# Gate tiles dealt earlier and tied behind the weight tiles, their sums begun as the bias, and one tile for the high parts of the merged output

## The chip, the cores and the metric

The kernel runs on one core of a Trainium2 chip. The metric is the time of one execution on the device in microseconds. Three runs of the kernel before took 822.36 to 823.37 us, with a median of 822.74 us.

## The reference

One decoder layer over a sequence of 256 tokens with 2048 channels, in float32. An input vector c gives a shift, a scale and a gate; the normalised input goes through a wide projection; two token mixers run beside each other; their outputs are projected, merged and projected out:

```python
ada = c @ w_ada + b_ada
shift, scale, gate = jnp.split(ada, 3, axis=-1)
h = rms_norm(x, g_pre) * (1.0 + scale[:, None, :]) + shift[:, None, :]
proj = h @ w_in                                    # 2048 x 11824
(qa, kc, vc, ks, vs, kw, vw, ga, za, qb, kb, vb, zb, ma, mb) = jnp.split(proj, IN_SPLITS, axis=-1)
oa = nsa_attention(...)                            # mixer A: 16 heads of 64, three branches
ya = (oa * jax.nn.silu(za)) @ w_br_a               # 1024 x 2048
ob = dilated_mixture(...)                          # mixer B: 8 heads of 128
yb = (ob * jax.nn.silu(zb)) @ w_br_b               # 1024 x 2048
merged = jax.nn.sigmoid(ma) * ya + jax.nn.sigmoid(mb) * yb
out = merged @ w_out                               # 2048 x 2048
return x + gate[:, None, :] * rms_norm(out, g_post)
```

The change touches three places of it: gate (a third of c @ w_ada + b_ada, needed only at the end), merged as an operand of the last product, and the loads of g_post and x for the last line.

## The kernel before

**Products in two parts.** Each float32 operand of a large product is split into a high part and a low part, which TensorE multiplies in its fp32r type: high by high, low by high, high by low. Of the weights ScalarE writes the high part (wH) and VectorE the low part (wL = raw - wH), lines 490 and 491.

**Items.** All weights are cut into items, tiles of 512 KB in most stages, in one list in the order in which TensorE uses them: the passes of the input projection (its last panels are ma and mb, 512 columns each), then the branch stage (w_br_a and w_br_b in turn, one quarter of the columns after the other), then w_out. An item of 512 columns and 256 rows is 12 products of 128x512. `dma(i)` asks for an item's tile on SyncE's queue, in one of seven buffers (raw); `prep(i)` writes wH and wL, three items ahead of the products in `main(i)`. Each prepared item asks for the tile seven further on.

**Gate items.** The gate vector is not a product on TensorE: 32 tiles of w_ada (two halves of 1024 columns, 16 tiles each) are multiplied on VectorE by c, one number per partition, and summed in gacc0 and gacc1 (lines 509 and 511). The first tile of a half is written by a TENSOR_SCALAR, the 15 others are added by a SCALAR_TENSOR_TENSOR. `spread` deals these items between the weight items from `late` on, here from the last four items of mb. When a half is done, GpSimd adds the bias (bg) to its first row (line 1142); near the end a product with ones sums gacc over the partitions (g_ps), and the result is multiplied into gp, the copies of g_post in all partitions.

**The side work.** Attention and everything else that is no item is a generator, `side_main`, of which a step is taken at each weight item. `need` makes it run on to a named point. mixer B's softmaxes lie in it (lines 1040 to 1080), then y, the mixers' outputs times their SiLU gates, split in yH and yL. In the branch stage it takes the merged quarters: for each quarter and each half of the tokens (t) TensorE transposes four blocks into a PSUM buffer, m_ps (one buffer, line 1115), ScalarE copies the high parts (mH, line 1121), and VectorE writes the low parts (mL, line 1122). Here mH lies in seven tiles (`Parts`, of 1 to 4 blocks each) and mL in one. Then ScalarE issues the loads of gp, bg and xr (x again, for the residual), lines 1132 to 1136.

**What sets the order.** The program is written in this order, but the instructions of each engine are then placed by a scheduler, which puts each as early as it expects its inputs. `behind(...)` (tc.issue_after) keeps an instruction in its place behind others. Each engine's queue is then fixed: an instruction that waits holds up all that stand behind it on its engine.

Of the kernel before, what the change touches and what calls it, by code (L numbers as in the profile page):

```python
# [48 lines left out]
def _build(ctx, tc, x, c, positions, w_ada, b_ada, g_pre, g_post, w_in, pe_ck, pe_cv, w_ck1, w_ck2,  # L49
# [396 lines left out]
    late = len(items) - 4  # L446
# [31 lines left out]
    gacc = {}  # L478

    def prep(i):  # L480
# [5 lines left out]
        if it.kind in ("w", "ck"):  # L486
# [4 lines left out]
            V.tensor_tensor(L, raw, H.bitcast(F32), op=OP.subtract)  # L491
            it.H, it.L = H, L
            return
        if it.kind == "ada":
            if it.kt0 == 0:
                accs[it.piece] = ST[:, len(accs) % 2].rearrange("p (h n) -> p h n", h=2)
            acc = accs[it.piece][:, :, :it.n // 2]
        else:
            if it.half not in gacc:
                need("A")  # L500
                gacc[it.half] = big.tile([128, 1024], F32, name=f"gacc{it.half}", tag=("cv", "k2")[it.half])
            acc = gacc[it.half]
        with behind(*(first_h if i < 8 else ())):
            for j in range(it.nk):
# [3 lines left out]
                if it.kt0 + j == 0:  # L508
# [194 lines left out]
    def side_main():  # L703
# [320 lines left out]

        while ("vb", 512) not in done:
            yield
# [76 lines left out]
        mH, mL = Parts(), big.tile([128, KT, S], F32R, name="mL", tag="xH")  # L1103
        for a, b in groups:
            mH.put(lows(a, b, "mH", F32R), a, b)
        yT["m"] = (mH, mL)
        for p in range(4):
# [4 lines left out]
            for t in range(NT):  # L1112
# [3 lines left out]
                ts = slice(t * 128, (t + 1) * 128)  # L1116
                for a, b in groups:
                    a, b = max(a, 4 * p), min(b, 4 * p + 4)
                    if a < b:
                        dH, o = mH.at[a]  # L1120
                        A.activation(dH[:, a - o:b - o, ts], ps[:, a - 4 * p:b - 4 * p], AF.Copy, scale=0.5)
                        V.scalar_tensor_tensor(mL[:, a:b, ts], ps[:, a - 4 * p:b - 4 * p], 0.5,
                                               dH[:, a - o:b - o, ts].bitcast(F32), op0=OP.mult, op1=OP.subtract)
                if t == NT - 1:
                    done.add(("mT", p))
                yield
# [5 lines left out]
        A.dma_start(gp, bass.AP(tensor=g_post.tensor, offset=g_post.offset, ap=[[0, 128], [1, D]]))  # L1132
        bg = big.tile([1, D], F32, name="bg", tag="qb")
        A.dma_start(bg, b_ada[0:1, 2 * D:3 * D])
        for t in range(NT):
            A.dma_start(fin["x"][:, t, :], x[0, t * 128:(t + 1) * 128, :])
# [3 lines left out]
        for half in range(2):  # L1140
            ga = gacc[half]
            G.tensor_tensor(ga[0:1, :], ga[0:1, :], bg[:, half * 1024:(half + 1) * 1024], op=OP.add)
# [89 lines left out]
```

## Time and profile before

| | |
|---|---|
| median of three runs | 822.74 us |
| the profiled execution, its own time | 823.46 us |
| its span, first to last instruction | 821.6 us |
| busy in the span: TensorE | 791.5 us, 96% |
| VectorE | 688.7 us, 84% |
| ScalarE | 417.3 us, 51% |
| GpSimd | 92.0 us, 11% |
| mean granted TensorE clock | 0.994 of full speed |
| traffic of the DMA engines | 193.26 MB, 235 GB/s on average |

In the rows PE is TensorE, PEld its weight loads, DVE VectorE, ACT ScalarE, POOL GpSimd and SP SyncE, whose queue issues the tile loads; a q behind the name is the engine's queue of instructions that don't compute. L560 is line 560 of the kernel. An instruction is named by what it writes and reads: wL<-raw,wH writes wL. The mb panels run from about 520 to 630 us, the branch stage from there to 722 us, w_out from there to 812 us. A wait that the rows name is idle time of that engine before the instruction, with what ended it.

### The profile page before, as it was taken

The page shows a single profiled execution, that of the slowest core. Times are in us where ns is not written, and L with a number is a line of the kernel's source. Part 1 is how long each engine was busy: PE and PEld are TensorE (multiplying, and loading weights), DVE is VectorE, ACT ScalarE, POOL GpSimd, SP SyncE. Part 2 cuts the span into 40 slices and gives each one's busy share as a digit, 9 for nine tenths or more (in the row PEclk, how much of TensorE's full clock was granted, in tenths as well). Part 3 has the DMA queues.
Part 4 walks back from the last instruction along what each step waited for, and adds up shares of the span by engine and source line. Part 5 has one row for each costly group of instructions (what it writes and reads, how often), then busy time and mean ns, then how long its engine had stood idle before and what let it go on. Part 6 is the DMA issues. An engine that isn't in the chain of part 4 may idle for free.

```text
span 821.6 us, 11929 instructions
## 1 busy us (share of the span) xinstructions
PE 791.5 (96%) x4160; PEld 665.9 (81%) x4160; DVE 688.7 (84%) x1068; ACT 417.3 (51%) x684; POOL 92.0 (11%) x111
## 2 busy tenths in 40 slices
PE   5999999999999999999999999999999999999995
PEld 4587888899888888888889999888878878888884
DVE  4899999999997979898888998867568999967455
ACT  2763363433334656576766666556644344445441
POOL 4200000000000036054511120011000010100000
PEclk9999999999999999999999999999999999999998
DMA  9999899989798558744444436554469989986633
GB/s 327 289 349 316 262 332 308 344 295 347 256 337 294 172 160 281 233 122 144 136 141 120 141 113 180 179 154 130 152 237 358 334 290 342 335 272 228 191 101 103
DMA packets 106950, 193.26 MB, mean 235 GB/s; under 512 B 7593, under 2 KB 36617, under 8 KB 106249
## 3 DMA queue, kind: packets, MB, share of 16 engines
q1 hardware_dynamic: 105376, 189.17, 69.5%
q10 hardware_dynamic: 1514, 3.33, 1.1%
q8 instruction: 33, 0.54, 0.3%
q14 instruction: 27, 0.22, 0.1%
HBM read 190.38 MB, written 2.10 MB: 234 GB/s over the span
## 4 chain that ended last, share of the span: by engine, by line
PE 84%; DVE 10%; issue 3%; DMA 2%; ACT 1%; DVEq 0%; ACTq 0%; SPq 0%
PE mm L560 21%; PE mm L561 21%; PE mm L563 21%; DVE wL L491 3%; PE mm L555 3%; PE mm L552 3%; PE mm L550 3%; PE mm L542 2%; PE pt_ps L923 1%; DVE ST L511 1%; PE sA L887 1%; DMA raw<-in_w_ada_dram 1%; PE ada_ps L184 1%; DMA xs<-in_x_dram 1%; PE pvb_ps L1058 1%
## 5 line engine op out<-in xcount | busy, mean ns | idle before, releaser
L490 ACT ACTIVATE wH<-raw 128x1024 fp32r<-128x1024 f32 (+2 forms) x268 | 267.4, 1000 | 293.0 <-PE mm L561 186.5
L491 DVE TENSOR_TENSOR wL<-raw,wH 128x1024 fp32r<-128x1024 f32 (+2 forms) x268 | 316.9, 1186 | 75.5 <-ACT wH L490 70.9
L560 PE MATMUL mm<-wH,xH 128*128 128x512 f32 (+2 forms) x616 | 237.8, 389 | 1.3 <-DVE KB L633 1.1
L561 PE MATMUL mm<-wH,xL 128*128 128x512 f32 (+2 forms) x616 | 235.0, 383 | 0.0
L563 PE MATMUL mm<-wL,xH 128*128 128x512 f32 (+2 forms) x616 | 188.6, 383 | 1.8 <-DVE wL L491 1.8
L560 PEld LDWEIGHTS mm<-wH,xH 128*128 128x128 f32 x616 | 116.1, 189 | 23.1 <-issue 2.7
L563 PEld LDWEIGHTS mm<-wL,xH 128*128 128x128 f32 x616 | 113.7, 189 | 24.2 <-DVE wL L491 2.5
L561 PEld LDWEIGHTS mm<-wH,xL 128*128 128x128 f32 x616 | 116.3, 189 | 20.5 <-DVE xL L246 0.3
L511 DVE SCALAR_TENSOR_TENSOR ST<-raw,vecT,ST 128x768 f32<-128x768 f32 (+2 forms) x75 | 75.9, 1013 | 1.3 <-DMA raw<-in_w_ada_dram 0.9
L550 PE MATMUL mm<-xH,wH 128*128 128x256 f32 x240 | 62.2, 280 | 1.1 <-DVE VB L633 1.1
L552 PE MATMUL mm<-xL,wH 128*128 128x256 f32 x240 | 61.7, 278 | 0.0
L560 PE MATMUL mm<-wH,yH 128*128 128x512 f32 x128 | 50.2, 392 | 0.0
L561 PE MATMUL mm<-wH,yL 128*128 128x512 f32 x128 | 50.0, 390 | 0.0
L561 PE MATMUL mm<-wH,mL 128*128 128x512 f32 x128 | 49.9, 390 | 0.0
L560 PE MATMUL mm<-wH,mH 128*128 128x512 f32 x128 | 49.9, 390 | 0.0
L555 PE MATMUL mm<-xH,wL 128*128 128x256 f32 x240 | 49.1, 280 | 0.6 <-DVE wL L491 0.6
L550 PEld LDWEIGHTS mm<-xH,wH 128*128 128x128 f32 x240 | 45.0, 188 | 1.7 <-issue 1.7
L511 DVE SCALAR_TENSOR_TENSOR gacc<-raw,vecT,gacc 128x1024 f32<-128x1024 f32 x30 | 38.3, 1278 | 8.9 <-DMA raw<-in_w_ada_dram 8.9
L552 PEld LDWEIGHTS mm<-xL,wH 128*128 128x128 f32 x240 | 45.0, 188 | 0.0
L563 PE MATMUL mm<-wL,mH 128*128 128x512 f32 x128 | 39.8, 389 | 0.0
L563 PE MATMUL mm<-wL,yH 128*128 128x512 f32 x128 | 39.5, 390 | 0.0
L555 PEld LDWEIGHTS mm<-xH,wL 128*128 128x128 f32 x240 | 37.0, 188 | 1.0 <-DVE wL L491 1.0
(296 smaller groups left out, 1002.4 us busy)
## 6 DMA issues: line engine op xcount, KB each, us to landing
raw<-in_w_in_dram SPq DMA_DIRECT2D x165, 512.0 KB, 4.2
raw<-in_w_ada_dram SPq DMA_DIRECT2D x48, 512.0 KB, 5.6
raw<-in_w_ada_dram SPq DMA_DIRECT2D x48, 384.0 KB, 4.7
raw<-in_w_out_dram SPq DMA_DIRECT2D x32, 512.0 KB, 4.8
raw<-in_w_br_a_dram SPq DMA_DIRECT2D x16, 512.0 KB, 5.7
raw<-in_w_br_b_dram SPq DMA_DIRECT2D x16, 512.0 KB, 5.9
raw<-in_w_in_dram SPq DMA_DIRECT2D x29, 256.0 KB, 2.7
raw<-in_w_ada_dram SPq DMA_DIRECT2D x24, 256.0 KB, 4.8
```

Source lines behind the costliest of these rows:

```text
L184: T.matmul(ada0[:, half, j, :], lhsT=raws0[q][:, kk, half, j * 128:(j + 1) * 128], rhs=cT[:, kt:kt + 1].to_broadcast([128, 128]), start=(k ...
L490: A.activation(H, raw, AF.Copy)
L491: V.tensor_tensor(L, raw, H.bitcast(F32), op=OP.subtract)
L511: V.scalar_tensor_tensor(acc, r, cc, acc, op0=OP.mult, op1=OP.add)
L542: T.matmul(job.ps[t][:, :job.n], lhsT=hj[:, t * 128:(t + 1) * 128], rhs=it.raw[:, j, cs], start=(first and j == 0), stop=(last and j == it ...
L550: T.matmul(ps, lhsT=it.H[:, j, bs], rhs=sH[:, it.kt0 + j, :], start=(first and j == 0 and b == 0), stop=False, skip_group_check=True)
L552: T.matmul(ps, lhsT=it.H[:, j, bs], rhs=sL[:, it.kt0 + j, :], start=False, stop=False, skip_group_check=True)
L555: T.matmul(ps, lhsT=it.L[:, j, bs], rhs=sH[:, it.kt0 + j, :], start=False, stop=(last and j == it.nk - 1), skip_group_check=True)
L560: T.matmul(ps, lhsT=sH[:, it.kt0 + j, ts], rhs=it.H[:, j, cs], start=(first and j == 0), stop=False)
L561: T.matmul(ps, lhsT=sL[:, it.kt0 + j, ts], rhs=it.H[:, j, cs], start=False, stop=False)
L563: T.matmul(ps, lhsT=sH[:, it.kt0 + j, ts], rhs=it.L[:, j, cs], start=False, stop=(last and j == it.nk - 1))
L887: T.matmul(o, lhsT=QT[:, u.t, h // 2, h % 2, :], rhs=KTt[:, hl, :, 0:128] if u.t == 0 else KTt[:, hl, u.br, :], start=(hl == 0), stop=(hl ...
```

## The change

Four things change.

- The gate items are dealt from 24 items before the end of the projection on, which is the second panel of mb, instead of from the last 4 items. The 32 tiles then lie between 56 weight items, before between 36.
- Each gate sum is kept behind the last wL that was written before it (`lowest`).
- gacc0 and gacc1 are cleared on GpSimd after mixer A, and the bias is loaded into their first rows; all 32 sums are then SCALAR_TENSOR_TENSOR, and GpSimd's two bias adds and the tile bg are gone.
- The high parts of merged are one tile, copied by one instruction for four blocks; the low parts lie in the seven tiles. The load of gp is kept behind the high part of the second quarter, that of xr behind that of the fourth.

```diff
@@ -443,7 +443,7 @@
                 it.kind, it.which, it.q, it.nk, it.n = "ck", n - 3, q, 4, 256
                 it.src = rows((w_ck1, w_cv1)[n - 3][0], 4 * q, 4, 0, 256)
                 items.append(it)
-    late = len(items) - 4
+    late = len(items) - 24
 
     yT = {}
     ws = []
@@ -476,6 +476,7 @@
             DMA.dma_start(it.raw, it.src)
 
     gacc = {}
+    lowest = [None]
 
     def prep(i):
         it = items[i]
@@ -488,7 +489,7 @@
             H, L = (wp.tile([128, 1152], F32R, name="w" + x, tag="w" + x, bufs=3)[:, o:o + it.nk * it.n].rearrange(
                 "p (k n) -> p k n", k=it.nk) for x in "HL")
             A.activation(H, raw, AF.Copy)
-            V.tensor_tensor(L, raw, H.bitcast(F32), op=OP.subtract)
+            lowest[0] = V.tensor_tensor(L, raw, H.bitcast(F32), op=OP.subtract)
             it.H, it.L = H, L
             return
         if it.kind == "ada":
@@ -496,16 +497,14 @@
                 accs[it.piece] = ST[:, len(accs) % 2].rearrange("p (h n) -> p h n", h=2)
             acc = accs[it.piece][:, :, :it.n // 2]
         else:
-            if it.half not in gacc:
-                need("A")
-                gacc[it.half] = big.tile([128, 1024], F32, name=f"gacc{it.half}", tag=("cv", "k2")[it.half])
+            need("gacc")
             acc = gacc[it.half]
-        with behind(*(first_h if i < 8 else ())):
+        with behind(*(first_h if i < 8 else lowest if it.kind == "gate" else ())):
             for j in range(it.nk):
                 cc, r = cT[:, it.kt0 + j:it.kt0 + j + 1], raw[:, j, :]
                 if it.kind == "ada":
                     r = r.rearrange("p (h n) -> p h n", h=2)
-                if it.kt0 + j == 0:
+                if it.kt0 + j == 0 and it.kind == "ada":
                     V.tensor_scalar(acc, r, cc, None, op0=OP.mult)
                 else:
                     V.scalar_tensor_tensor(acc, r, cc, acc, op0=OP.mult, op1=OP.add)
@@ -1022,6 +1021,12 @@
                 V.tensor_tensor(d, ps[:, :, t, :], d, op=OP.add)
             yield
 
+        for half in range(2):
+            gacc[half] = big.tile([128, 1024], F32, name=f"gacc{half}", tag=("cv", "k2")[half])
+            G.memset(gacc[half], 0.0)
+            A.dma_start(gacc[half][0:1, :], b_ada[0:1, 2 * D + half * 1024:2 * D + (half + 1) * 1024])
+        done.add("gacc")
+
         while ("vb", 512) not in done:
             yield
         for t in range(NT):
@@ -1100,9 +1105,10 @@
 
         while ("merged", 0) not in done:
             yield
-        mH, mL = Parts(), big.tile([128, KT, S], F32R, name="mL", tag="xH")
+        mH, mL = big.tile([128, KT, S], F32R, name="mH", tag="xH"), Parts()
         for a, b in groups:
-            mH.put(lows(a, b, "mH", F32R), a, b)
+            mL.put(lows(a, b, "mL", F32R), a, b)
+        turned = []
         yT["m"] = (mH, mL)
         for p in range(4):
             while ("merged", p) not in done:
@@ -1114,32 +1120,33 @@
                 for j in range(4):
                     T.transpose(ps[:, j, :], MA[:, t, (4 * p + j) * 128:(4 * p + j + 1) * 128], ident)
                 ts = slice(t * 128, (t + 1) * 128)
+                dH = mH[:, 4 * p:4 * p + 4, ts]
+                last = A.activation(dH, ps, AF.Copy, scale=0.5)
                 for a, b in groups:
                     a, b = max(a, 4 * p), min(b, 4 * p + 4)
                     if a < b:
-                        dH, o = mH.at[a]
-                        A.activation(dH[:, a - o:b - o, ts], ps[:, a - 4 * p:b - 4 * p], AF.Copy, scale=0.5)
-                        V.scalar_tensor_tensor(mL[:, a:b, ts], ps[:, a - 4 * p:b - 4 * p], 0.5,
-                                               dH[:, a - o:b - o, ts].bitcast(F32), op0=OP.mult, op1=OP.subtract)
+                        dL, o = mL.at[a]
+                        V.scalar_tensor_tensor(dL[:, a - o:b - o, ts], ps[:, a - 4 * p:b - 4 * p], 0.5,
+                                               dH[:, a - 4 * p:b - 4 * p].bitcast(F32), op0=OP.mult, op1=OP.subtract)
                 if t == NT - 1:
                     done.add(("mT", p))
+                    turned.append(last)
                 yield
 
         fin["o"] = big.tile([128, NT, D], F32, name="og", tag="mb")
         fin["x"] = big.tile([128, NT, D], F32, name="xr", tag="ma")
         fin["ssq"] = const.tile([128, NT, 4], F32, name="ssq2")
         gp = big.tile([128, D], F32, name="gp", tag="zb")
-        A.dma_start(gp, bass.AP(tensor=g_post.tensor, offset=g_post.offset, ap=[[0, 128], [1, D]]))
-        bg = big.tile([1, D], F32, name="bg", tag="qb")
-        A.dma_start(bg, b_ada[0:1, 2 * D:3 * D])
-        for t in range(NT):
-            A.dma_start(fin["x"][:, t, :], x[0, t * 128:(t + 1) * 128, :])
+        with behind(turned[1]):
+            A.dma_start(gp, bass.AP(tensor=g_post.tensor, offset=g_post.offset, ap=[[0, 128], [1, D]]))
+        with behind(turned[3]):
+            for t in range(NT):
+                A.dma_start(fin["x"][:, t, :], x[0, t * 128:(t + 1) * 128, :])
         yield
         while "gate" not in done:
             yield
         for half in range(2):
             ga = gacc[half]
-            G.tensor_tensor(ga[0:1, :], ga[0:1, :], bg[:, half * 1024:(half + 1) * 1024], op=OP.add)
             gH, gL = (wp.tile([128, 1152], F32R, name="g" + v, tag="w" + v, bufs=3)[:, :1024] for v in "HL")
             A.activation(gH, ga, AF.Copy)
             V.tensor_tensor(gL, ga, gH.bitcast(F32), op=OP.subtract)
```

Three places show how the instructions move. The first is VectorE's queue at the end of the mb panels. gacc0 is the gate's first half, wL a low part of a weight tile, yL a low part of a mixer's output; raw buffers have higher numbers the later they were asked for. Before:

```order
L509 TENSOR_SCALAR gacc0_6339<-raw_6188,vecT_98 128x1024
L1097 SCALAR_TENSOR_TENSOR yL1_6335<-ZB_178,yH1_6334 128x512 x3
L491 TENSOR_TENSOR wL_6227<-raw_6068,wH_6226 128x1024
L491 TENSOR_TENSOR wL_6250<-raw_6086,wH_6249 128x1024
L511 SCALAR_TENSOR_TENSOR gacc0_6339<-raw_6230,vecT_98,gacc0_6339 128x1024
L491 TENSOR_TENSOR wL_6271<-raw_6119,wH_6270 128x1024
L511 SCALAR_TENSOR_TENSOR gacc0_6339<-raw_6274,vecT_98,gacc0_6339 128x1024
L491 TENSOR_TENSOR wL_6294<-raw_6139,wH_6293 128x1024
L491 TENSOR_TENSOR wL_6317<-raw_6170,wH_6316 128x1024
```

And in the changed kernel:

```order
L492 TENSOR_TENSOR wL_6324<-raw_6230,wH_6323 128x1024
L1102 SCALAR_TENSOR_TENSOR yL1_6389<-ZB_178,yH1_6388 128x512 x3
L492 TENSOR_TENSOR wL_6347<-raw_6245,wH_6346 128x1024
L510 SCALAR_TENSOR_TENSOR gacc0_5629<-raw_6257,vecT_98,gacc0_5629 128x1024
L492 TENSOR_TENSOR wL_6371<-raw_6272,wH_6370 128x1024
L492 TENSOR_TENSOR wL_6394<-raw_6290,wH_6393 128x1024
L510 SCALAR_TENSOR_TENSOR gacc0_5629<-raw_6301,vecT_98,gacc0_5629 128x1024
L492 TENSOR_TENSOR wL_6418<-raw_6318,wH_6417 128x1024
L510 SCALAR_TENSOR_TENSOR gacc0_5629<-raw_6327,vecT_98,gacc0_5629 128x1024
```

Before, the sum of raw_6274 stands ahead of the low parts of raw_6139 and raw_6170, which were asked for earlier; now each sum stands behind the low part of the tile asked for just before its own, and the first half has no TENSOR_SCALAR.

The second place is VectorE's queue at the first quarter of merged. mL are the low parts, m_ps the PSUM buffer of the transposes, MA the merged values. Before:

```order
L491 TENSOR_TENSOR wL_6721<-raw_6619,wH_6720 128x1024
L1122 SCALAR_TENSOR_TENSOR mL_6643<-m_ps_6694,mH0_6644 128x128
L511 SCALAR_TENSOR_TENSOR gacc0_6339<-raw_6641,vecT_98,gacc0_6339 128x1024
L1122 SCALAR_TENSOR_TENSOR mL_6643<-m_ps_6694,mH1_6645 128x2x128
L509 TENSOR_SCALAR gacc1_6780<-raw_6674,vecT_98 128x1024
L1122 SCALAR_TENSOR_TENSOR mL_6643<-m_ps_6694,mH3_6646 128x128
L644 SCALAR_TENSOR_TENSOR MA_179<-MA_179,mm_6653 128x512
L491 TENSOR_TENSOR wL_6755<-raw_6651,wH_6754 128x1024
L1122 SCALAR_TENSOR_TENSOR mL_6643<-m_ps_6726,mH0_6644 128x128
```

And in the changed kernel:

```order
L492 TENSOR_TENSOR wL_6730<-raw_6627,wH_6729 128x1024
L1129 SCALAR_TENSOR_TENSOR mL0_6673<-m_ps_6720,mH_6672 128x128
L1129 SCALAR_TENSOR_TENSOR mL1_6674<-m_ps_6720,mH_6672 128x2x128
L1129 SCALAR_TENSOR_TENSOR mL3_6675<-m_ps_6720,mH_6672 128x128
L510 SCALAR_TENSOR_TENSOR gacc1_5632<-raw_6633,vecT_98,gacc1_5632 128x1024
L492 TENSOR_TENSOR wL_6774<-raw_6651,wH_6773 128x1024
L1129 SCALAR_TENSOR_TENSOR mL0_6673<-m_ps_6747,mH_6672 128x128
L1129 SCALAR_TENSOR_TENSOR mL1_6674<-m_ps_6747,mH_6672 128x2x128
L1129 SCALAR_TENSOR_TENSOR mL3_6675<-m_ps_6747,mH_6672 128x128
```

Before, a gate sum and the first product of the second half stood between the three low parts of one buffer; now the three stand in a row, with a sum behind them. On TensorE ten rows, one item's products, stand between the first and the second transposes of each quarter now; before it was 17, 14, 11 and 11 rows.

The third place is ScalarE's queue near 449 us, in mixer A. AR are the keys, split from PSUM (k_ps), gacc is a gate tile of sums, and the DMA row is the load of a bias. Before:

```order
L490 ACTIVATE wH<-raw 128x1024
L846 ACTIVATE AR<-k_ps 64x256
L847 ACTIVATE AR<-k_ps 64x256
L490 ACTIVATE wH<-raw 128x1024
L846 ACTIVATE AR<-k_ps 64x256
L847 ACTIVATE AR<-k_ps 64x256
L927 ACTIVATE PH<-pt_ps 128x512
```

And in the changed kernel:

```order
L491 ACTIVATE wH<-raw 128x1024
L845 ACTIVATE AR<-k_ps 64x256
L846 ACTIVATE AR<-k_ps 64x256
L1027 DMA gacc_5632<-in_b_ada_dram 1x1024
L845 ACTIVATE AR<-k_ps 64x256
L846 ACTIVATE AR<-k_ps 64x256
L491 ACTIVATE wH<-raw 128x1024
```

A bias load stands between the two pairs of evictions, and it waits for GpSimd's memset of the same tile; the wH that stood there is behind the second pair.

## Rows read from the trace of the kernel before

**Rows 1.** The page, part 1: busy time, share of the span, instructions

```profile
PE 791.5 (96%) x4160; PEld 665.9 (81%) x4160; DVE 688.7 (84%) x1068; ACT 417.3 (51%) x684; POOL 92.0 (11%) x111
```

**Rows 2.** TensorE's waits, 500 to 822 us: total, times, longest

```profile
PE mm L563 <- DVE wL L491: 1.8, 1, 1.8
PE m_ps L1115 <- DVE mL L1122: 1.6, 1, 1.6
```

**Rows 3.** Stretches: us, PE, PEld, DVE, ACT, POOL busy, clock, DMA share, GB/s

```profile
614.00:616.00 2.00, 0.21 (x1) 0.21 (x2) 2.00 (x3) 0.00 (x0) 0.00 (x0) 1.00 0.14 44
616.00:618.00 2.00, 2.00 (x7) 1.58 (x7) 2.00 (x3) 0.02 (x1) 0.00 (x0) 0.68 0.93 279
618.00:620.00 2.00, 2.00 (x6) 1.54 (x6) 1.20 (x2) 1.04 (x1) 0.00 (x0) 0.50 0.83 309
```

**Rows 4.** VectorE's timeline: start, duration, instruction, idle time before it

```profile
599.76 0.74 DVE L509 TENSOR_SCALAR gacc<-raw,vecT 128x1024 f32<-128x1024 f32 x1
...
605.24 1.28 DVE L511 SCALAR_TENSOR_TENSOR gacc<-raw,vecT,gacc 128x1024 f32<-128x1024 f32 x1 [0.66 <-DMA raw<-in_w_ada_dram]
...
613.31 1.28 DVE L511 SCALAR_TENSOR_TENSOR gacc<-raw,vecT,gacc 128x1024 f32<-128x1024 f32 x1 [5.65 <-DMA raw<-in_w_ada_dram]
614.51 2.35 DVE L491 TENSOR_TENSOR wL<-raw,wH 128x1024 fp32r<-128x1024 f32 x2
```

**Rows 5.** The chain that ended last: start, duration, what

```profile
604.61 8.60 DMA raw<-in_w_ada_dram
```

**Rows 6.** ScalarE's timeline at gp, and transfers: KB each, us to landing

```profile
603.67 0.36 ACTq L1132 DMA_DIRECT2D gp<-in_g_post_dram  x1
...
raw<-in_w_ada_dram SPq DMA_DIRECT2D x48, 512.0 KB, 5.6
...
gp<-in_g_post_dram ACTq DMA_DIRECT2D x1, 1024.0 KB, 7.8
```

**Rows 7.** Timelines of VectorE and GpSimd at 661 us

```profile
661.16 2.75 DVE L509 TENSOR_SCALAR gacc<-raw,vecT 128x1024 f32<-128x1024 f32 x1
...
660.99 2.37 POOL L1142 TENSOR_TENSOR gacc<-gacc,bg 1x1024 f32<-1x1024 f32 x1 [82.69 <-DVE gacc L511]
```

**Rows 8.** Stretch 620 to 630 us, columns as in rows 3

```profile
620.00:630.00 10.00, 10.00 (x45) 8.27 (x44) 8.73 (x8) 3.80 (x5) 0.00 (x0) 0.99 0.98 356
```

**Rows 9.** Two earlier stretches, columns as in rows 3

```profile
100.00:200.00 100.00, 100.00 (x561) 87.47 (x560) 98.54 (x126) 44.48 (x49) 0.00 (x0) 1.00 0.95 320
540.00:580.00 40.00, 40.00 (x208) 34.00 (x207) 30.48 (x62) 25.03 (x43) 6.24 (x6) 1.00 0.46 142
```

**Rows 10.** Groups from 600 to 740 us: busy us, mean ns, idle before

```profile
L491 DVE TENSOR_TENSOR wL<-raw,wH 128x1024 fp32r<-128x1024 f32 x48 | 59.7, 1247 | 9.2 <-ACT wH L490 8.8
L511 DVE SCALAR_TENSOR_TENSOR gacc<-raw,vecT,gacc 128x1024 f32<-128x1024 f32 x30 | 38.3, 1278 | 8.9 <-DMA raw<-in_w_ada_dram 8.9
...
L1122 DVE SCALAR_TENSOR_TENSOR mL<-m_ps,mH 128x256 fp32r<-128x256 f32 x6 | 2.5, 414 | 0.2 <-ACT mH L1121 0.2
...
L623 ACT ACTIVATE MB<-mm 128x512 f32<-128x512 f32 x4 | 2.3, 587 | 1.5 <-PE mm L563 1.5
```

**Rows 11.** Around 449 us: GpSimd, ScalarE, TensorE; and GpSimd's memsets

```profile
448.24 1.04 POOL L918 TENSOR_TENSOR P<-P,cf 128x512 f32<-128x512 f32 x1 [3.60 <-DVE cf L916]
...
451.28 0.38 ACT L846 ACTIVATE AR<-k_ps 64x256 fp32r<-64x256 f32 x1 [0.78 <-DVE AR L849]
...
453.55 0.63 PE L923 MATMUL pt_ps<-ident,P 128*128 128x128 f32 x4 [0.90 <-DVE AR L849]
...
L752 POOL MEMSET BL<- 128x32 f32 x4 | 0.6, 155 | 252.4 <-DVE BL L756 241.9 <-DVE mf L302 10.5
```

**Rows 12.** The third quarter's transposes (TensorE) and first copy (ScalarE)

```profile
704.75 0.60 PE L1115 MATMUL m_ps<-ident,MA 128*128 128x128 f32 x4
...
708.19 0.60 PE L1115 MATMUL m_ps<-ident,MA 128*128 128x128 f32 x4
...
705.46 0.36 ACT L1121 ACTIVATE mH<-m_ps 128x256 fp32r<-128x256 f32 x1
```

## The prediction

> **What bounds the kernel now.** I read the page first: TensorE is busy for 791.5 us of a span of 821.6 us [rows 1]. What it lacks lies mostly in the load at the start and the last normalisation, which the change leaves alone, so the question is where it stands still in between. The list of TensorE's waits from 500 us on has two rows: 1.8 us for a low part (wL) and 1.6 us for a low part of the merged output [rows 2]. Both lie in the stretch that the change rewrites. [...]
>
> The first wait. VectorE's timeline [rows 4] shows its cause. The gate sum of 613.31 had waited 5.65 us for its tile, and the two low parts of 614.51 stood behind it, the first of them the one TensorE waited for. The chain of waits gives the tile: issued at 604.61, landed 8.60 us later [rows 5]. One microsecond before it, at 603.67, ScalarE had issued gp, a transfer of 1 MB [rows 6]. The gate tile is no late item of the queue: by its number it was dealt after the two low parts that stand behind it (first pair of listings in the section on the change). So it was taken about as soon as it was expected, and blocked work that was ready. A standstill of 5.65 us cost TensorE 1.79 us, so the first 3.9 us or so were covered by the items already prepared.
>
> The second wait. At 661.16 the first product of the second gate half, a TENSOR_SCALAR, takes 2.75 us, beside GpSimd's bias add of 660.99, which takes 2.37 us [rows 7]; the same instruction alone took 0.74 us [rows 4]. It stands between the low parts of the first quarter, whose PSUM buffer TensorE wants back.
>
> **The change part by part.** *Dealing and tying.* 32 gate tiles went over 36 weight items and go over 56, and each sum is queued behind the last wL before it. The sum of 613.31 can then no longer stand ahead of low parts dealt before it; a tile is used in the order in which it was asked for, seven tiles later. In the branch stage an item is 12 products, and 45 products fill 10 us [rows 8], so 2.67 us an item and 32/56 of a gate tile with each: seven tiles are 7/1.57 x 2.67 = 11.9 us, against 8.60 us for the slowest landing here. The traffic there, 1.57 x 0.524 MB in 2.67 us, is 308 GB/s, where before it ran at 356 GB/s and 0.98 of the engines [rows 8]. And gp is issued behind the second quarter's high part, so it no longer meets the first gate tiles. I take off the wait of 1.79 us, and the clock lost after it: 2 x (1 - 0.68) + 2 x (1 - 0.50) = 1.64 us [rows 3]. What is late next: nothing that the list of waits shows, until the second wait.
>
> The price is on VectorE. Seven sums now stand among the softmaxes of mixer B, by the order of its queue. There it was busy 30.48 of 40 us [rows 9]; 7 x 1.28 [rows 10] make it 39.4 of 40. That is nearly full, but from 100 to 200 us VectorE ran at 98.5% with TensorE never idle [rows 9], and 3.9 us are covered. I put it at 0. The other end: each of the six GpSimd products of that stretch (1.04 us, as the row of 448.24) holds up one sum, 6.2 us more, 5.7 us behind in all; less the cover, 1.8 us of idle TensorE.
>
> *Sums that begin as the bias.* Two TENSOR_SCALAR (0.74 and 2.75 us) become two sums of 1.28 us, and GpSimd's adds and the bg load go: 0.9 us less on VectorE, and with the 2.75 us goes its collision, so the second wait of 1.62 us. Added are two GpSimd memsets and two bias loads on ScalarE's queue. The first load stands between two evictions of k_ps near 449 us (third pair of listings), and ScalarE stops there until the memset is done; queued behind it are the evictions, a wH and all that follows. No row here is a memset of that size. It starts behind the product of 448.24, which ends at 449.28. From below it takes 0.15 us (128x32); from above twice the 1.04 us that a product of half its length took, ending at 451.4 [rows 11]. ScalarE's next eviction started only at 451.28, kept back by VectorE [rows 11]. So the delay is between nothing and 0.12 us plus the issue, 0.36 us for gp's [rows 6]: 0 to 0.5 us, of which I take 0.2, the middle, since no row is near. TensorE waits 0.90 us there at 453.55 for the same evictions [rows 11]; as VectorE's operations there are reordered too, that wait may also go, which I keep for the lower end. The second memset comes after the last product of mixer A, with GpSimd idle, and costs nothing.
>
> What the memset does to VectorE beside it: the TENSOR_SCALAR of [rows 7] was held for its GpSimd neighbour's whole run, so by the nearest row a neighbour could cost up to 2 us. [...]
>
> *High parts in one tile.* ScalarE's 18 copies become 8 of 128x512, and the low parts, in pieces, no longer take turns with them; at VectorE's busiest the pieces stand in a row (second pair of listings). ScalarE is half idle, so the shorter work itself is worth 0. It matters for how soon the one PSUM buffer comes free for the second four transposes of a quarter: copy starts 0.71 us after the transposes, 0.59 us for a copy of that size (MB's), three pieces of at most 0.41 us, 2.54 us together, where the third quarter had 3.44 us between its transposes without a wait [rows 10, 12]. After the change one item's products stand between them in every quarter, as there. I take 0.
>
> **The sum.** 1.79 + 1.64 + 1.62 - 0.2 = 4.85 us off the profiled execution's 823.46 us (span 821.6): 818.6 us. That execution lies 0.72 us above the median of the three runs, 822.74, so I forecast 817.9 us.
>
> **The rivals.**
> *The first wait comes back elsewhere.* Three ways, one price: the gap and its clock, 3.43 us, so 821.3 us. (a) VectorE too full in mixer B, as priced above (1.8 us of gap). For it: 39.4 of 40; against it: the stretch at 98.5%. (b) gp now lands in the branch stage, where 308 of 356 GB/s are wanted: its 1.05 MB take 2.9 us of the engines, on top of the 5.6 us from issue to landing that a gate tile takes [rows 6], 8.5 us in all, within the 11.9 us. [...] (c) The tie doesn't do what it says, and sums still block low parts for other reasons.
> *Slower.* The one PSUM buffer of the quarters. Where a wL (1.25 us) and a gate sum (1.28 us) stand ahead of the pieces, it comes free after 2.54 + 2.53 = 5.07 us, 1.63 us too late; in all four quarters 6.5 us, and one fall of the clock as in [rows 3] makes 8.1: 822.74 - 4.85 + 8.1 = 826.0 us. It decides from 1.2 us a quarter. For it: the first quarter has lost slack, over one and a half items' products before and one item's now; against it: the third quarter, and the order, in which the pieces follow each other.
>
> **Chances.** Forecast 0.67, its own range 816.4 to 819.0; (a) 0.12, (b) 0.08, (c) 0.06; the slower one 0.07. A measurement of this kernel can tell about 0.2% from no change, 1.6 us, so faster means under 821.1. The three at 821.3 lie on that line, half of them on each side: faster 0.80, same 0.14, slower 0.06 (the milder form of the last counts as same). The range: below, the memset at nothing (0.2), the 0.90 us at 453.55 gone, and 0.4 us for the fastest run under the median: 816.4, rounded to 816.3. Above, the three at 821.3 with 0.4 us of spread: 821.7.
>
> **What would show it.** Right: no TensorE wait of over 1 us between 600 and 740 us, granted clock 1.00 throughout, gate sums without a wait for their tile, VectorE below 9 tenths from 640 us on. Wrong: a wait of TensorE for wL between 545 and 600 us (a), at 685 to 700 us (b), or a row m_ps in the list of waits (the slower one); an idle ScalarE near 449 us longer than 1 us means that the memset is dearer than I took it for.

## The result and the profile after

The changed kernel takes 818.52 us (median of 6 runs, 817.75 to 819.52); the kernel before took 823.06 us beside it (6 runs, 821.81 to 824.26). The ratio is 0.9942, with an interval of [0.9928, 0.9956]: faster by 4.5 us, where 4.85 us were forecast, and 0.6 us above the forecast time.

Its page, part 1, answers to [rows 1]:

```profile
span 817.0 us, 11914 instructions
...
PE 790.0 (97%) x4160; PEld 666.3 (82%) x4160; DVE 686.2 (84%) x1068; ACT 414.9 (51%) x674; POOL 88.8 (11%) x111
```

The span is 4.6 us shorter. Where they came from is seen when both spans are cut in three; first the kernel before, then the changed one (columns as in rows 3):

```profile
0.00:600.00 600.00, 582.40 (x3235) 494.73 (x3236) 522.80 (x884) 324.97 (x569) 86.34 (x109) 1.00 0.70 227
600.00:700.00 100.00, 96.59 (x426) 79.09 (x425) 87.44 (x90) 41.15 (x49) 2.37 (x1) 0.98 0.91 321
700.00:821.60 121.60, 112.46 (x502) 92.10 (x500) 78.50 (x96) 51.19 (x68) 3.31 (x1) 0.97 0.60 203
```

```profile
0.00:600.00 600.00, 582.40 (x3232) 495.14 (x3233) 530.62 (x888) 322.95 (x568) 88.81 (x111) 1.00 0.72 235
600.00:700.00 100.00, 100.00 (x452) 82.86 (x451) 84.59 (x94) 43.36 (x46) 0.00 (x0) 1.00 0.90 302
700.00:817.00 117.00, 107.58 (x480) 88.33 (x478) 71.03 (x88) 48.61 (x61) 0.00 (x0) 0.98 0.57 189
```

TensorE's idle time up to 600 us is the same to the hundredth, 17.60 us. From 600 to 700 us it falls from 3.41 us to nothing, and 3.41 is the sum of the two waits of [rows 2]. From 700 us on it is 9.42 us instead of 9.14. The rest is TensorE's busy time, 791.45 us before and 789.98 after: 1.47 us, where the lower clock of [rows 3] was put at 1.64. 3.41 - 0.28 + 1.47 = 4.6. These are two executions; the executions of the kernel before differ by 2.5 us among themselves.

The list of TensorE's waits from 500 to 822 us, two rows in [rows 2], is empty, and VectorE has room in the stretch in which it was full (620:640 answers to [rows 8], 540:580 to [rows 9]):

```profile
540.00:580.00 40.00, 40.00 (x206) 34.05 (x205) 35.04 (x63) 23.10 (x39) 6.03 (x5) 1.00 0.68 216
600.00:620.00 20.00, 20.00 (x90) 16.58 (x89) 18.20 (x20) 10.05 (x11) 0.00 (x0) 1.00 0.85 279
620.00:640.00 20.00, 20.00 (x90) 16.58 (x89) 14.53 (x14) 8.57 (x10) 0.00 (x0) 1.00 0.92 296
640.00:660.00 20.00, 20.00 (x94) 16.57 (x93) 17.49 (x22) 8.41 (x9) 0.00 (x0) 1.00 0.88 299
```

The groups from 600 to 740 us, which answer to [rows 10], say the same from VectorE's side. Its sums are idle before by 0.0 us instead of 8.9, and its low parts wait only for their high parts, so VectorE is now ahead of its work and not behind it:

```profile
L492 DVE TENSOR_TENSOR wL<-raw,wH 128x1024 fp32r<-128x1024 f32 x49 | 59.8, 1222 | 26.5 <-ACT wH L491 26.5
L510 DVE SCALAR_TENSOR_TENSOR gacc<-raw,vecT,gacc 128x1024 f32<-128x1024 f32 x22 | 28.1, 1277 | 0.0
...
L1124 ACT ACTIVATE mH<-m_ps 128x512 fp32r<-128x512 f32 x8 | 4.6, 580 | 0.0
```

### The profile page after: what moved, and what is told of

Its sections match the earlier page's. It is cut to its first block, busy times and chain, and to the rows that moved or that the text cites. A ratio compares the mean times of both kernels' runs of the same rounds, so it can differ in the third digit from the quotient of the medians.

```text
span 817.0 us, 11914 instructions
## 1 busy us (share of the span) xinstructions
PE 790.0 (97%) x4160; PEld 666.3 (82%) x4160; DVE 686.2 (84%) x1068; ACT 414.9 (51%) x674; POOL 88.8 (11%) x111
## 4 chain that ended last, share of the span: by engine, by line
PE 85%; DVE 9%; issue 2%; ACT 2%; DMA 1%; DVEq 0%; ACTq 0%; SPq 0%
PE mm L559 22%; PE mm L560 22%; PE mm L562 21%; DVE wL L492 3%; PE mm L554 2%; PE mm L549 2%; PE mm L551 2%; PE mm L541 2%; DVE ST L510 2%; PE pt_ps L922 1%; PE sA L886 1%; PE ada_ps L184 1%; DMA xs<-in_x_dram 1%; PE pvb_ps L1063 1%; ACT wH L491 1%
## 5 line engine op out<-in xcount | busy, mean ns | idle before, releaser
L510 DVE SCALAR_TENSOR_TENSOR gacc<-raw,vecT,gacc 128x1024 f32<-128x1024 f32 x32 | 41.0, 1282 | 0.0
L562 PE MATMUL mm<-wL,yH 128*128 128x512 f32 x128 | 39.4, 390 | 0.0
```

Source lines behind the costliest of these rows:

```text
L510: V.scalar_tensor_tensor(acc, r, cc, acc, op0=OP.mult, op1=OP.add)
L562: T.matmul(ps, lhsT=sH[:, it.kt0 + j, ts], rhs=it.L[:, j, cs], start=False, stop=(last and j == it.nk - 1))
```

## The experiments

**The theories.** *Blocked queue*: the sums stood on VectorE's queue ahead of low parts whose tiles had been asked for earlier; the tie ends that, and the rest matters little. *Traffic*: tiles land late because the transfers crowd in the branch stage (with gp among them); dealing earlier and holding gp end that. *Collision*: the second wait is the TENSOR_SCALAR beside GpSimd's bias add, and beginning with the bias ends it. One number is read from VectorE's queue for every version: how many low parts of tiles asked for earlier stand behind each of the 32 sums. In the kernel before it is 5, 4, 4, 3, 3 for the first five and 2 to 0 for the rest; in the changed kernel it is 0 for all.

### The parts one by one

The tie alone, on the kernel before:

```diff
-            V.tensor_tensor(L, raw, H.bitcast(F32), op=OP.subtract)
+            lowest[0] = V.tensor_tensor(L, raw, H.bitcast(F32), op=OP.subtract)
...
-        with behind(*(first_h if i < 8 else ())):
+        with behind(*(first_h if i < 8 else lowest if it.kind == "gate" else ())):
```

> The kernel before, with the tie alone: each gate sum behind the last wL written before it; dealing from the last four items of mb, gp issued early, TENSOR_SCALAR and bias adds as before. Queue theory (the first wait comes from sums that stand ahead of low parts of tiles asked for earlier): no sum waits over 3 us for its tile, TensorE's wait at 614 us and the fallen clock after it are gone, 3.4 us off the kernel before (about 819.5 us); the wait for m_ps may stay. [...]

Dealing from the second panel of mb on alone:

```diff
-    late = len(items) - 4
+    late = len(items) - 24
```

> The kernel before, with the dealing alone: gate items from 24 items before the end of the projection on, not tied. By the order 30 of 32 sums stand ahead of 4 or 5 low parts of tiles asked for earlier. Queue theory: the sums wait for their tiles again and again (over 10 us of VectorE's waits for gate tiles in all), TensorE waits for wL in several places, no gain: 822 us or more. Traffic theory: at 308 GB/s instead of 356 the tiles land in time, the first wait is gone, 3.4 us off: about 819.5 us.

Holding the loads of gp and xr alone:

```diff
+        with behind(turned[1]):
             A.dma_start(gp, bass.AP(tensor=g_post.tensor, offset=g_post.offset, ap=[[0, 128], [1, D]]))
```

> The kernel before, with gp and xr alone held behind the second and the fourth quarter of merged. Queue theory: the sums still stand ahead of 3 to 5 low parts, but the gate tile of 604 us no longer shares the engines with gp and lands about 2.9 us sooner, so VectorE waits 2.7 us, which 3.9 us of cover hide: first wait gone, 3.4 us off, about 819.5 us. Traffic theory in the form that the dense dealing is what matters: the wait stays at 1 us or more.

And the changed kernel without the tie:

```diff
-        with behind(*(first_h if i < 8 else lowest if it.kind == "gate" else ())):
+        with behind(*(first_h if i < 8 else ())):
```

> The changed kernel without the tie: sums placed by the scheduler, which puts them ahead of 4 or 5 low parts asked for earlier. Queue theory: VectorE waits for gate tiles, TensorE for wL, 2 us or more above the changed kernel: 820.5 us or more. Traffic theory: as the changed kernel, 818.5 us within 0.7.

| | median us | ratio to before |
|---|---|---|
| tie alone | 818.71 | 0.9945 [0.9924, 0.9966] |
| dealing alone | 845.28 | 1.026 [1.0232, 1.0288] |
| gp and xr held alone | 822.14 | 0.9988 [0.997, 1.0007] |
| changed, without the tie | 837.94 | 1.0175 [1.015, 1.02] |

The tie alone is the whole gain: its list of TensorE's waits from 500 to 735 us is empty (the wait for m_ps, which might have stayed, is gone too), and its granted clock from 600 to 700 us is 1.00. The dealing without it costs 2.6%, since the scheduler then puts each sum 5 or 4 low parts ahead. The waits of VectorE for gate tiles and of TensorE, 500 to 740 us, with dealing alone:

```profile
DVE gacc L511 <- DMA raw<-in_w_ada_dram: 39.2, 24, 4.9
...
PE mm L563 <- DVE wL L491: 8.7, 6, 3.3
PE m_ps L1115 <- DVE mL L1122: 8.1, 2, 5.3
```

The traffic theory falls by the same rows: from 600 to 700 us this version moved 251 GB/s with a DMA share of 0.77, the kernel before 321 GB/s with 0.91, and it waited four times as long (39.2 us against 8.9). Lower traffic is in part what waiting leaves, but its gate tiles landed sooner, too: 4.4 us against 5.9, the medians of those asked for from 630 to 740 us. The tie alone ran that stretch at 330 GB/s and 0.94 without one wait for a gate tile.

With gp held alone VectorE's longest wait for a gate tile was 2.8 us, as expected (2.7), and TensorE's first wait and its clock, 3.43 us, were gone (the clock was 1.00 from 600 to 650 us); but the second wait grew from 1.6 to 2.8 us, and the clock fell to 0.50 after it in its turn (TensorE's timeline, then two stretches of it). The execution shown took 826.05 us, the second slowest of ten (820.54 to 826.25), so it doesn't show the median one. Nor is it shown that the hold of gp ended the first wait: the version with the bias start alone, below, loads gp as the kernel before does, and its execution has no first wait either.

```profile
665.07 1.03 PE L1116 MATMUL m_ps<-ident,MA 128*128 128x128 f32 x4 [2.78 <-DVE mL L1123]
```

```profile
664.00:666.00 2.00, 0.93 (x5) 0.96 (x6) 2.00 (x4) 0.00 (x0) 0.00 (x0) 0.79 0.97 372
666.00:668.00 2.00, 2.00 (x6) 1.55 (x6) 1.93 (x5) 0.66 (x2) 0.00 (x0) 0.50 0.83 213
```

### The second wait

Sums that begin as the bias, alone on the kernel before (GpSimd's adds and bg go as in the change):

```diff
-                if it.kt0 + j == 0:
+                if it.kt0 + j == 0 and it.kind == "ada":
...
+            G.memset(gacc[half], 0.0)
+            A.dma_start(gacc[half][0:1, :], b_ada[0:1, 2 * D + half * 1024:2 * D + (half + 1) * 1024])
```

> The kernel before with one part: gacc cleared and started as the bias, all 32 sums of one kind, GpSimd's two bias adds and the load of bg gone; dealing, order rule, high parts and the load of gp as before. Theory (blocked queue): the first wait of about 1.8 us and its clock stay, since on VectorE's queue sums still stand ahead of up to five low parts of tiles asked for earlier; the second wait of 1.62 us goes with the TENSOR_SCALAR that took 2.75 us beside GpSimd's add: 1.6 us less than before, about 822.0 us. Rival (places on the queue, not that collision, make the second wait): a low part of a weight and a gate sum now stand between the pieces of one quarter, and a row m_ps of over 1 us stays in TensorE's waits: within 0.7 us of before. The memsets: no idle ScalarE of over 1 us near 449 us.

The high parts in one tile, alone:

```diff
-        mH, mL = Parts(), big.tile([128, KT, S], F32R, name="mL", tag="xH")
+        mH, mL = big.tile([128, KT, S], F32R, name="mH", tag="xH"), Parts()
```

> The kernel before with one part: the high parts of merged in one tile, copied four blocks at once, the low parts in seven tiles; all else as before. Theory: the first wait stays, about 1.8 us and its clock. On VectorE's queue the pieces of the low parts of a quarter now stand in a row and the first product of the second half stands behind the first quarter's pieces: if the collision with GpSimd's add was the second wait, it happens still but elsewhere and costs TensorE nothing: 1.6 us less than before, about 822.0 us. Rival: the collision costs its 1.6 us wherever it stands, as before within 0.7 us. Slower rival of the prediction: a row m_ps of over 1 us a quarter and 3 us or more above before.

And the changed kernel with the TENSOR_SCALAR and GpSimd's adds put back:

```diff
+            G.tensor_tensor(ga[0:1, :], ga[0:1, :], bg[:, half * 1024:(half + 1) * 1024], op=OP.add)
```

> The changed kernel with the bias added as before: a TENSOR_SCALAR as first product of each half, GpSimd's two bias adds, no memsets. By the working of the prediction (the collision of the TENSOR_SCALAR with GpSimd's add is the second wait): an instruction of VectorE of over 2 us beside each bias add, and TensorE waits 1.6 us again: about 820.1 us. By the blocked queue theory: the collision is still there, but nothing behind it on the queue has been blocked before, so the items prepared ahead cover it: as the changed kernel, within 0.7 us of 818.5 us.

Measured: bias alone 825.02 us (1.0023 [1.0008, 1.0037]), slower than before; one tile alone 820.63 us (0.9961 [0.9947, 0.9975]), over half of the gain, where 822.0 was expected of both; the changed kernel without the bias start 818.93 us (0.9942 [0.9925, 0.9959]), as the changed one.

The collision is not all there is to the second wait. With the bias start alone there is no GpSimd add and no TENSOR_SCALAR, and the second wait is longer than before; the first wait, which was expected to stay, is not in this execution:

```profile
PE m_ps L1119 <- DVE mL L1126: 3.1, 2, 2.9
```

VectorE's timeline of this version shows why. (A piece is one instruction that writes low parts of merged, mL.) The transposes began at 655.10, but VectorE was still at earlier work, reached the first piece 4.28 us later, and a low part and a sum stand between the pieces, as the rival in the expectation said:

```profile
659.38 0.29 DVE L1126 SCALAR_TENSOR_TENSOR mL<-m_ps,mH 128x128 fp32r<-128x128 f32 x1
659.58 1.22 DVE L491 TENSOR_TENSOR wL<-raw,wH 128x1024 fp32r<-128x1024 f32 x1
660.71 0.42 DVE L1126 SCALAR_TENSOR_TENSOR mL<-m_ps,mH 128x256 fp32r<-128x256 f32 x1
661.04 1.27 DVE L509 SCALAR_TENSOR_TENSOR gacc<-raw,vecT,gacc 128x1024 f32<-128x1024 f32 x1
662.24 0.28 DVE L1126 SCALAR_TENSOR_TENSOR mL<-m_ps,mH 128x128 fp32r<-128x128 f32 x1
```

The kernel before, read in the same way (TensorE's transposes, then VectorE's first and last piece):

```profile
657.46 0.60 PE L1115 MATMUL m_ps<-ident,MA 128*128 128x128 f32 x4
664.26 0.63 PE L1115 MATMUL m_ps<-ident,MA 128*128 128x128 f32 x4 [1.62 <-DVE mL L1122]
...
659.43 0.28 DVE L1122 SCALAR_TENSOR_TENSOR mL<-m_ps,mH 128x128 fp32r<-128x128 f32 x1
...
663.83 0.28 DVE L1122 SCALAR_TENSOR_TENSOR mL<-m_ps,mH 128x128 fp32r<-128x128 f32 x1
```

Here VectorE reached the first piece 1.97 us after the transposes began, the pieces took 4.68 us to the end of the last, and TensorE wanted the buffer 5.18 us after the transposes began. Of the 4.68 us the collision of [rows 7] was 2.01 (2.75 instead of 0.74), more than the 1.62 us of the wait: with all else unchanged, the wait would have gone with it. With the bias start alone all else did change: the pieces took 1.54 us less, but VectorE came to them 2.31 us later after the transposes, and TensorE wanted the buffer 0.47 us sooner; 1.62 - 1.54 + 2.31 + 0.47 = 2.86. In the time of the span VectorE came no later (659.38 against 659.43). It was TensorE that came sooner, by 2.36 us, in an execution without the first wait. So in the kernel before the first wait hid part of VectorE's lateness; this is read from one execution of each.

The tie alone changes VectorE's side (TensorE, then VectorE):

```profile
654.48 0.60 PE L1116 MATMUL m_ps<-ident,MA 128*128 128x128 f32 x4
659.96 0.60 PE L1116 MATMUL m_ps<-ident,MA 128*128 128x128 f32 x4
...
656.56 0.29 DVE L1123 SCALAR_TENSOR_TENSOR mL<-m_ps,mH 128x128 fp32r<-128x128 f32 x1
...
659.42 0.29 DVE L1123 SCALAR_TENSOR_TENSOR mL<-m_ps,mH 128x128 fp32r<-128x128 f32 x1
```

VectorE reached the first piece nearly 3 us sooner than in the kernel before (656.56), and the last ended 5.23 us after the transposes began, just before TensorE took the buffer again without a wait. GpSimd's add is still there, at 659.59, but the TENSOR_SCALAR has moved behind the second half's pieces (665.45), so no collision falls between these pieces.

With the adds put back into the changed kernel the collision is there, at full price, and TensorE has no wait (VectorE, then GpSimd): two low parts take 4.39 us where two usually take 2.35. But it ends over 20 us before the first quarter's pieces (657.08); what one between the pieces would cost under the tie, this run does not show.

```profile
631.42 4.39 DVE L492 TENSOR_TENSOR wL<-raw,wH 128x1024 fp32r<-128x1024 f32 x2 [0.30 <-ACT wH L491]
```

```profile
631.20 2.39 POOL L1148 TENSOR_TENSOR gacc<-gacc,bg 1x1024 f32<-1x1024 f32 x1 [47.91 <-DVE gacc L512]
```

One tile alone left both waits, but smaller, 1.1 us for a wL and 1.2 us for m_ps, and the clock stayed at 1.00 after both; that makes up its gain (2.3 us in its profile's span). So pieces that stand in a row don't end the second wait by themselves. The first wait lies 40 us ahead of any piece, and why it was smaller here no run shows. Why the bias start alone came out 0.2% slower than before stays open: its profiled run was its fastest of ten (823.22 us), so the profile doesn't show what the median one paid.

### Dealing, gp and the dose of the tie

The changed kernel with the tiles dealt over the last 36 items as before, and with gp issued early as before:

```diff
-    late = len(items) - 24
+    late = len(items) - 4
```

> The changed kernel with the 32 gate tiles dealt over the last 36 weight items as before, with all else of the change, the tie among it. Theory (blocked queue): once each sum stands behind the low part before it, a tile landing late holds up nothing that was asked for earlier: as the changed kernel, within 0.7 us of 818.5 us, although 0.89 of a gate tile instead of 0.57 goes with each weight item. Rival (traffic): the transfers at 350 GB/s and more land late, VectorE's sums wait for tiles and TensorE for wL: 820 us or more.

```diff
-        with behind(turned[1]):
+        if True:
             A.dma_start(gp, bass.AP(tensor=g_post.tensor
```

> The changed kernel with the load of gp not kept behind the second quarter, so that ScalarE issues it at the start of the branch stage as before. Blocked queue theory: gp's 1 MB meets gate tiles again and some land in over 8 us, but the sums stand behind the low parts asked for earlier and have 11.9 us: as the changed kernel, within 0.7 us of 818.5 us, no TensorE wait of over 1 us from 600 us on. Rival (the hold of gp is part of the gain): a gate sum waits for its tile beside gp, TensorE waits for wL: 820 us or more.

819.08 us (0.9945 [0.9927, 0.9963]) and 818.26 us (0.9947 [0.9928, 0.9967]): both as the changed kernel, with an empty list of TensorE's waits from 500 to 735 us. Under the tie neither the dealing nor the hold of gp matters. Then the tie one, two and three low parts further back (here two; `lowest` is the list of all low parts written so far):

```diff
-        with behind(*(first_h if i < 8 else lowest if it.kind == "gate" else ())):
+        with behind(*(first_h if i < 8 else lowest[-3:-2 or None] if it.kind == "gate" else ())):
```

> The changed kernel with each gate sum tied behind the last wL but one, so that exactly one low part of a tile asked for earlier stands behind each sum (the changed kernel has none, the kernel before up to five). Blocked queue theory, by the working of the prediction: a tile then has 11.9 - 2.67 = 9.2 us from asking to use, more than the slowest landing of 8.6 us: no loss, within 0.7 us of 818.5 us. Rival (any sum ahead of an older low part costs): 820 us or more.

> The changed kernel with each gate sum tied two low parts further back. Blocked queue theory: 11.9 - 5.3 = 6.6 us from asking to use, above the median landing of 5.6 us and below the slowest: some sums wait for their tile, up to 2 us, below the 3.9 us that prepared items cover: 818.5 to 820.5 us. Rival (a threshold lies elsewhere, so that the theory's 11.9 us is wrong): as the changed kernel without a single wait for a tile, or 823 us and more.

> The changed kernel with each gate sum tied three low parts further back. Blocked queue theory: 11.9 - 8.0 = 3.9 us from asking to use, less than the 5.6 us of a median landing: nearly every sum waits for its tile, 1 to 2 us each, some 25 us or more in all, over the spare time of VectorE from 600 to 740 us (about 21 us of 140): slower than the changed kernel by 2 to 12 us, 820.5 to 830.5 us. Rival (only the four and five low parts of the version without the tie hurt): within 0.7 us of 818.5 us.

The table pairs each gate tile's issue on SyncE's queue with the start of its sum, in order, 32 pairs a version; the time between is the median of the pairs after 630 us (15 or 16 of them), the landing the median of the gate tiles asked for from 630 to 740 us (14 or 15).

| older low parts behind each sum | from asking to use, us | landing, us | waits for a gate tile | median us | ratio to before |
|---|---|---|---|---|---|
| 0 (the changed kernel) | 11.4 | 5.7 | none | 818.52 | 0.9942 [0.9928, 0.9956] |
| 1 | 9.4 | 5.3 | none | 818.04 | 0.9946 [0.9929, 0.9964] |
| 2 | 7.9 | 6.1 | 1.4 us in 1 | 819.26 | 0.9956 [0.9942, 0.997] |
| 3 | 5.8 | 5.6 | 4.6 us in 6 | 819.63 | 0.996 [0.9945, 0.9974] |
| 5 or 4 (without the tie) | 4.6 | 4.5 | 42.8 us in 26 | 837.94 | 1.0175 [1.015, 1.02] |

One and two came out at the times expected. Three was expected at 820.5 to 830.5 us and came out at 819.63: a step takes about 1.9 us from the time (11.4 to 5.8 in three), not 2.67. The rows show the reason. With three, the sum of the 18th tile starts 7.80 us earlier than in the changed kernel, but the tile is also asked for 1.76 us earlier (SyncE's queue and VectorE, changed kernel first):

```profile
626.78 0.34 SPq L476 DMA_DIRECT2D raw<-in_w_ada_dram  x1
...
638.15 1.28 DVE L510 SCALAR_TENSOR_TENSOR gacc<-raw,vecT,gacc 128x1024 f32<-128x1024 f32 x1
```

```profile
625.02 0.34 SPq L476 DMA_DIRECT2D raw<-in_w_ada_dram  x1
...
630.35 1.28 DVE L510 SCALAR_TENSOR_TENSOR gacc<-raw,vecT,gacc 128x1024 f32<-128x1024 f32 x1
```

I take it that earlier sums free their buffers earlier, and so bring the asking forward; no run separates that. The waits begin where the time from asking to use comes down to the landing. At 5.8 against 5.6 us six sums waited; that kernel is about a microsecond above the changed one, within the intervals. Without the tie 26 of the 32 sums waited, so the 4.6 us there are the landing itself (4.5 us), and how far below it the order would go can't be read from them; this costs 19.4 us. No version that was run beats the changed kernel beyond the intervals.

## Why the prediction was right, step by step

- **The first wait, 1.79 us, and its clock, 1.64 us.** Right in size: both waits are gone, and TensorE's busy time fell by 1.47 us. The reason was the blocked queue, and here the prediction shared the credit wrongly: dealing earlier and holding gp were put beside the tie, but the tie does it alone, and the dealing without it is the slower kernel. The 11.9 us from asking to use, worked out from the branch stage's items, measured 11.4.
- **The second wait, 1.62 us.** Right in size, incomplete in its cause. The step "with the 2.75 us goes its collision, so the second wait" fits the rows of the kernel before, where the collision took 2.01 us of a wait of 1.62. But it priced the two waits as independent of each other, and they are not: the bias start alone, in an execution without the first wait, waited 2.86 us, and gp held alone 2.78. In every version with the tie TensorE has no such wait; alone, the tie brings VectorE to the first piece at 656.56 instead of 659.43. So both terms of the sum came from the tie, where the sum gave the second one to the bias start; that they could be added was luck. Under the tie the bias start is worth nothing that a run shows (818.93 us without it).
- **The memset, 0.2 us of 0 to 0.5.** Nothing that the rows show. It takes 0.95 us and ends at 450.53; the next eviction started at 451.64, kept back by VectorE as before ([rows 11]), and the wait of TensorE behind it was 0.82 us instead of 0.90, so that possible gain did not come either:

```profile
449.58 0.95 POOL L1026 MEMSET gacc<- 128x1024 f32 x1
...
451.64 0.38 ACT L845 ACTIVATE AR<-k_ps 64x256 fp32r<-64x256 f32 x1 [1.88 <-DVE AR L848]
...
453.71 0.63 PE L922 MATMUL pt_ps<-ident,P 128*128 128x128 f32 x4 [0.82 <-DVE AR L848]
```

- **VectorE beside the memsets.** By the row of [rows 7] the prediction allowed up to 2 us beside each, and its sum has no term for that. The low part beside the second memset (507.13, 0.95 us), which it overlapped for 0.51 us, took its usual 1.22 us. The one beside the first (449.58, 0.95 us) took 1.59 us, 0.37 us more, but it also overlapped the last 0.51 us of a GpSimd product (448.61, 1.04 us), so it doesn't show which of the two goes with that.

```profile
449.14 1.59 DVE L492 TENSOR_TENSOR wL<-raw,wH 128x1024 fp32r<-128x1024 f32 x1 [0.70 <-ACT wH L491]
...
507.57 1.22 DVE L492 TENSOR_TENSOR wL<-raw,wH 128x1024 fp32r<-128x1024 f32 x1
```

- **Mixer B on VectorE, put at 0.** Right: TensorE never idled there. 39.4 of 40 us were foretold and 35.04 came: six sums fell into the stretch and not seven, and other work moved behind it; from 600 to 620 us the low parts of y (yL) took 4.94 us instead of 1.89.
- **One tile, put at 0.** Under the tie nothing came from it that a run can show. The slack was thinner than worked out: the first quarter's second transposes come 3.21 us after the first (3.44 foretold), and the last piece ends 2.82 us after them (2.54 foretold), so 0.39 us are left (the row of 656.62 ends at 657.43):

```profile
654.61 0.60 PE L1121 MATMUL m_ps<-ident,MA 128*128 128x128 f32 x4
657.82 0.60 PE L1121 MATMUL m_ps<-ident,MA 128*128 128x128 f32 x4
```

```profile
656.62 0.81 DVE L1129 SCALAR_TENSOR_TENSOR mL<-m_ps,mH 128x128 fp32r<-128x128 f32 x3
```

- **The rivals.** (a) did not come, as just said. (b): gp was issued at 683.89, the stretch 680 to 700 us moved 348 GB/s, and no sum waited. (c) fell with the first experiment. The slower one, the single PSUM buffer of the quarters, did hold TensorE up elsewhere: it waited for m_ps in the kernel before (1.6 us) and in all five versions without the tie (1.2 to 8.1 us in all), in the new order of pieces too (1.2 us with one tile alone). In the changed kernel the buffer came free 0.39 us before it was wanted, as above, so it doesn't decide.
- **The forecast time, 0.6 us too low.** In the profiled executions 4.70 us came off (823.46 to 818.76), 0.15 less than summed. The larger part is the step to the median: the prediction took off 0.72 us, as the profiled execution of the kernel before lay that far above the median of three runs; the changed kernel's lies only 0.24 above its own.

## What to carry to other kernels

In the kernel before one gate sum that waited 5.65 us for its transfer held up the low parts behind it on VectorE's queue, and TensorE for 1.79 us ([rows 2, 4]). So look for instructions that need a transfer and stand ahead of ready work that others wait for; one ordering edge gave here the whole gain (818.71 us alone), and spreading the same transfers earlier without the edge made the kernel slower (845.28 us). For each such instruction compare the time from asking for its tile to its use with the time to landing: the waits here set in where the two met (5.8 against 5.6 us). When two waits follow each other on one engine, don't add their prices before asking what the second becomes when the engine no longer stands at the first: here it grew from 1.62 to 2.8 us.

## What the runs showed of the hardware that was not expected

The length of a wait didn't decide here whether the clock fell after it. After waits of 1.79 us ([rows 3]) and 2.78 us (gp held alone) the granted clock fell to 0.50; after the 1.62 us of the kernel before it was 1.00 again throughout (664 to 700 us), and after the 2.86 us of the bias start alone it stayed at 1.00 in all stretches, with TensorE idle for the whole of the first (columns as in rows 3):

```profile
660.00:662.00 2.00, 0.00 (x0) 0.00 (x0) 2.00 (x3) 0.92 (x3) 0.00 (x0) 1.00 0.81 251
662.00:664.00 2.00, 1.33 (x8) 1.23 (x9) 2.00 (x5) 0.69 (x3) 0.00 (x0) 1.00 1.06 265
664.00:666.00 2.00, 2.00 (x10) 1.63 (x10) 1.91 (x4) 1.58 (x3) 0.00 (x0) 1.00 0.85 328
```

What did decide it no run shows. The clock term of the sum, 1.64 us, was therefore safe only because the rows of the very wait that went showed it. And a low part of VectorE took longer beside a GpSimd add on a single partition (1x1024): with the tie alone, a low part of 2.85 us instead of 1.22 stands beside an add of 2.39 us that began at 659.59. The excess is most of what was left of the add when the low part began, 1.63 of 1.76 us; it was 2.01 of 2.20 us for the TENSOR_SCALAR of [rows 7], and 2.04 of 2.17 us for the two low parts of 631.42 in the changed kernel with the adds.

```profile
660.22 2.85 DVE L492 TENSOR_TENSOR wL<-raw,wH 128x1024 fp32r<-128x1024 f32 x1
```
